# The last layer's modulation vectors as side work of the recurrence instead of block 2's attentions

## The chip, the cores and the metric

The kernel runs on one core of a Trainium2 chip. The metric is the time of one execution in microseconds (us), as the device measures it; lower is better. The engines are named as the profile names them: PE is TensorE (PEld its weight loads), DVE is VectorE, ACT is ScalarE, POOL is GpSimd, SP is SyncE. SP, ACT and POOL also issue DMAs, each in its own order.

## The reference

Two transformer blocks of two layers each are computed in float32 on 256 tokens of width 1024. The second layer of block 1 is a recurrence over 256 context tokens and 256 latent tokens in two directions; the layers of block 2 are attentions followed by a mixture of experts (MoE). Every layer is modulated: a vector `c` is passed through silu and multiplied by a 1024 x 6144 matrix, and the six results of 1024 each shift, scale and gate the layer.

```python
def second_block(x, c, norm1_g, ..., ada_w, ada_b, ...):
    cs = jax.nn.silu(c)
    for l in range(DEPTH):
        mod = (cs @ ada_w[l] + ada_b[l])[:, None, :]
        sh1, sc1, g1, sh2, sc2, g2 = jnp.split(mod, 6, axis=-1)
        h = rms_norm_2(x, norm1_g[l]) * (1.0 + sc1) + sh1
        y = even_mixer_2(h, ...) if l % 2 == 0 else odd_mixer_2(h, ...)
        x = x + g1 * y
        h = rms_norm_2(x, norm2_g[l]) * (1.0 + sc2) + sh2
        x = x + g2 * hier_moe(h, ...)
    return rms_norm_2(x, final_g)
```

`mod` depends on `c` alone, so it can be computed at any time before its layer.

## The kernel before

The program goes through its layers one after the other: block 1's attention layer (`layer0`), the recurrence layer (`odd1`, then `mlp`, both called by `layer1`), and block 2 (`layerB(0)` with `even2`, `layerB(1)` with `odd2`, each followed by `moe`).

The modulation products are **side work**. A product of 512 columns is one unit (`ada_unit`, L191): its weights are 1024 x 512 numbers, 2 MB; eight matmuls of 128 rows each (L203) go to four groups of 32 columns of the PE array, so that up to four of them run side by side; ACT copies the four partial sums (L209); a small product with `sel2` adds them, as four pieces for a column result (L213) or as one for a row result (L217); DVE adds the bias (L255 or L271, and L273 for a norm weight). A layer of block 2 has 12 units (`ada2`, L1408): first four column units, then eight row units, whose results go to DRAM by POOL DMAs (L275).

A generator, `self.side`, yields after every two matmuls. `tick(n)` (L227) takes n such steps wherever the main work calls it, so a unit is four steps. In the recurrence `rw_feat` (L970, the features of two heads) and each of the four steps of `rw_chain` (L1165) call it, with the counts in the table `tk` (L1284). `causal_scores` (L1455) calls it in block 2's attentions. What is left of the generator is finished where `self.do(self.side)` stands: behind the last chain of the recurrence (L856) and in `layerB(1)` (L2005).

The weights come through a ring of buffers (`wload`, L149, and `self.weights(n)`), issued by SP in one order for the whole program. Inside the recurrence the ring has **two buffers of 512 KB** (`self.wn = 2`, `self.weights(2)`, L808 to L811), and the side work has one PSUM bank (`phase((3, 2, 1))`, L818). Behind the recurrence, at L884, a ring of eight buffers of 1 MB begins, which holds first `wo` (the recurrence layer's output matrix, 4 MB) and then the MLP's `w1` and `w2`; block 2 has ten such buffers.

The recurrence is done in four groups (g = 0 to 3), each with features, an inverse on DVE (`rw_inv`), products behind it (`rw_post2` for g = 3) and a chain of four dependent steps. Behind the last chain stand the readout of the second half of the heads (`rw_readout`, L931: a PE product L938, DVE and ACT steps, a PE product L955), the transposes of the result (L898), the product with `wo` (L187 to L189 with `moh`), the residual, and the MLP, which begins with L310.

The order of instructions on each engine is not the order of the code: a scheduler places them when the program is built, with its own estimate of the times. Each engine then runs its list strictly in that order.

Of the kernel before, what the change touches and what calls it, by code (L numbers as in the profile page):

```python
# [110 lines left out]
class K:  # L111
# [55 lines left out]
    def chain(self):  # L167

        prev = [None]

        def mm(*a, **k):
            i = self.nc.tensor.matmul(*a, **k)
            if prev[0] is not None:
                self.after(i, prev[0])
            prev[0] = i
            return i
        return mm
# [486 lines left out]
class L1(K):  # L664
# [21 lines left out]
    def odd1(self, xs, cst, Acol, Bcol):  # L686
# [131 lines left out]
        with self.phase((3, 2, 1), 0) as ph:  # L818
            self.pl = ph.es.enter_context(tc.tile_pool(name="pl", bufs=1, space=PSUM, reuse_waits="tile"))
            gp = ph.pool("gp")  # L820
            St = [self.T(gp, [P, 2, 4, P], f"St{c}") for c in range(2)]
            E3 = [self.T(gp, [P, 4, 65], f"E3{d}") for d in range(2)]
            for c in range(2):
                nc.gpsimd.memset(St[c], 0.0)
                nc.gpsimd.memset(E3[c][:, :, 64 * c:64 * c + 1], 1.0)
            E = dict(E3=E3, kT=kTd, kkn=kknd, rT=rTd, St=St, twl=twl, tal=tal, hpar=hpar, hka=hka, vd=vd,
                     ms=mstrict, mi=mincl, rmask=rmask, yd=yd, Y1=Y1, bon=bon, rkI=rkI, kbd=[self.tc.dram_tile([2, 4, P, 4, P], F32, name=f"kb_dram{g}") for g in range(4)],
                     ard=[self.tc.dram_tile([2, 4, P, 4, P], F32, name=f"ar_dram{g}") for g in range(2)],
                     rbd=[self.tc.dram_tile([2, 4, P, 8, 64], F32, name=f"rb_dram{g}") for g in range(2)])
            st = None  # L830
            self.nq = 4
            F = self.rw_open(0, False, gp)
            for hp in range(4):
                self.rw_feat(hp, gp, E, F)
            for g in range(4):
                N = {"hp": 0}

                def ahead(p):

                    while g < 3 and N["hp"] < 4 and self.pos[g][N["hp"]] <= p:  # L840
                        if N["hp"] == 0:
                            N["F"] = self.rw_open((g + 1) // 2, g % 2 == 0, gp)
                        self.rw_feat(N["hp"], gp, E, N["F"])
                        N["hp"] += 1
                ahead(0)
                self.rw_inv(gp, F)
                ahead(1)
                rest = (self.rw_post2 if g >= self.g2 else self.rw_post)(gp, F)
                st = self.rw_chain(gp, E, F, st, ahead, rest)
                ahead(9)  # L850
                F = N.get("F")
                if F:
                    Fl = F
            F = Fl

            self.do(self.side)  # L856
            E.update(z=z, J=J, sgl=sgl, behind=F["inv"])
            sl = slice(512, 1024)
            nc.gpsimd.dma_start(lng1, A["lng"][sl].partition_broadcast(P))
            nc.gpsimd.dma_start(g21, A["g2"][:, sl])  # L860
            t2 = lambda n: self.T(gp, [P, 512], n, bufs=3 if n in ("BK", "ARx") else 2)
            lng, lnb, g2 = (t2("BK") for _ in range(3))
            nc.gpsimd.dma_start(lng, A["lng"][0:512].partition_broadcast(P))
            nc.gpsimd.dma_start(lnb, A["lnb"][0:512].partition_broadcast(P))
            nc.gpsimd.dma_start(g2, A["g2"][:, 0:512])
            for t in range(2):
                rows = slice(t * P, (t + 1) * P)
                y, y1 = t2("KB"), t2("ARx")
                nc.scalar.dma_start(z[:, t, :], vd[0][rows, 0:512])
                nc.scalar.dma_start(y, yd[0][rows, :])  # L870
                nc.scalar.dma_start(y1, yd[1][rows, :])
                self.rw_bonus(0, t, E, z[:, t, :], lnb)
                self.rw_readout(t, E, y, y1, t2("RB"), lng, g2, z[:, t, :])
            lnb = t2("BK")
            nc.gpsimd.dma_start(lnb, A["lnb"][sl].partition_broadcast(P))
            for t in range(2):
                nc.scalar.dma_start(z1[:, t, :], vd[0][t * P:(t + 1) * P, sl])
                self.rw_bonus(1, t, E, z1[:, t, :], lnb)
# [402 lines left out]
    def q(self, n):  # L1281
        return getattr(self.nc, self.qs[n])

    tk = ((1, 0), (1, 0), (1, 0), (1, 0)), ((1, 2), (1, 2), (1, 2), (1, 2)), (4, 4, 2, 4)  # L1284
    late, g2 = 1, 3
    pos = ((3, 4, 9, 9), (9, 9, 9, 9), (4, 9, 9, 9), (5, 9, 9, 9))

    def layer1(self):
        nc = self.nc
        xs, cst = self.xs[:2], self.xs[2:]  # L1290
        self.at, self.side = "unit", chain(self.gates(1, 0), self.mods(1, 1), self.gates(1, 1), self.ada2(0))
        self.odd1(xs, cst, *self.modc[1, 0])
        self.early2()
        with self.phase() as ph:
            self.ar = ph.pool("ar1")
            self.ws = ph.pool("ws3", 2)
            self.mlp(xs, 1, *self.modc[1, 1], [0, 0], 1)
# [94 lines left out]
class B2(L1):  # L1392
# [600 lines left out]
    def layerB(self, l):  # L1993
        nc, A = self.nc, self.A
        xs = self.xs[:2]
        with self.phase() as ph:
            self.ar = ph.pool(f"arB{l}")
            self.ws = ph.pool(f"wsB{l}", 2)
            Ac, Bc = self.bmods[l]
            if l == 0:  # L2000
                self.at, self.side = "unit", self.ada2(1)
            hT = self.norm_mod_T(xs, Ac, Bc, [0, 0], rs=self.rn)
            mix = (self.even2 if l == 0 else self.odd2)(hT, ph)
            if l:
                self.do(self.side)  # L2005
            else:
                self.flush()
            G = self.T(self.ar, [P, D], "gates", bufs=1)
            self.row(G, f"bda{l}", 2, 0)
            logits = self.out2(mix, A["b_out"] if l == 0 else A["n_out"], xs, G, *self.router(l))  # L2010
        with self.phase(ns2=5) as ph:
            self.ar = ph.pool(f"arM{l}")
            hs = [self.T(self.ar, [P, 2, D], n, F32R) for n in ("mo_hh", "mo_hl")]
            xd = [self.T(self.ar, [P, KT, 256], "mo_xd", bufs=2) for _ in range(1)]
            hb = [self.T(self.ar, [P, D], f"mo_h{t}") for t in range(2)]
            rows = []
            for b in (4, 3, 5):
                rows.append(self.T(self.ar, [P, D], f"mo_row{b}"))
                self.row(rows[-1], f"bda{l}", b, 0)
            if l:  # L2020
                fg = self.T(self.ar, [P, D], "mo_fin")
                nc.gpsimd.dma_start(fg, A["fin_g"].partition_broadcast(P))
                self.fin = fg, hb
            self.rn = self.moe(xs, l, logits, rows, hb, *hs)
            if l:
                for t in range(2):
                    if t:
                        nc.vector.tensor_scalar(hb[t], hb[t], self.rn[t], None, ALU.mult)
                    else:
                        nc.scalar.activation(hb[t], hb[t], AF.Copy, scale=self.rn[t])  # L2030
                    nc.sync.dma_start(self.out[t * P:(t + 1) * P, :], hb[t])
# [54 lines left out]
```

## Time and profile before

| | us |
|---|---|
| median of 3 timed runs | 2259.72 (2257.11 to 2260.31) |
| the profiled execution, its own time | 2250.88 |
| its span, first to last instruction | 2248.9 |
| PE busy in the span | 2075.3 (92%) |
| DVE busy | 1159.6 (52%) |
| ACT busy | 856.6 (38%) |
| mean granted PE clock | 0.936 of 2.4 GHz |

A time of the timeline is counted from the first instruction. Busy shares are means over stages that differ much from each other. A matmul in float32 leaves two records in the trace, so the eight matmuls of a unit are 16 records.

### The profile page before, as it was taken

What the parts mean: (1) busy time and instruction counts of PE and PEld (TensorE: products, weight loads), DVE (VectorE), ACT (ScalarE), POOL (GpSimd) and SP (SyncE); (2) the same over time, 40 slices, a digit from 0 to 9 for tenths busy, and PEclk for the clock granted to TensorE, in tenths of its full rate; (3) what the DMA queues carried; (4) which work ended last, traced back from release to release, by engine and by line L of the source; (5) the groups of instructions that cost most, each with busy time, mean ns of one, the idle gap of its engine ahead of it and who ended that gap; (6) DMA issues with size and microseconds to landing.
All of it is one profiled execution on the core that took longest, in us unless ns stands there. A gap on an engine that the chain in (4) does not pass through costs nothing. (4 is left out here: it accounts for less than half of the span.)

```text
span 2248.9 us, 32827 instructions
## 1 busy us (share of the span) xinstructions
PE 2075.3 (92%) x13114; PEld 1451.2 (65%) x13114; DVE 1159.6 (52%) x2419; ACT 856.6 (38%) x1650; POOL 119.8 (5%) x216
## 2 busy tenths in 40 slices
PE   7999899999989989899997789998998989999897
PEld 4864688888866675685652569987765439646542
DVE  2247543433465536866826265666664236475433
ACT  3334443322352446564432345544452114243211
POOL 0100000000021000001111100000000000010000
PEclk9999999999999998759897889999998999999898
DMA  7448212222332426736886555537464959452494
GB/s 285 142 186 322 76 73 94 94 94 94 113 128 89 140 100 211 228 92 200 263 280 192 177 217 183 187 118 272 171 252 163 386 202 354 156 206 96 179 383 173
DMA packets 124310, 414.53 MB, mean 184 GB/s; under 512 B 20608, under 2 KB 59152, under 8 KB 88432
## 3 DMA queue, kind: packets, MB, share of 16 engines
q1 hardware_dynamic: 59824, 340.03, 41.1%
q10 hardware_dynamic: 55552, 50.95, 7.3%
q0 software_dynamic: 8768, 21.31, 3.1%
q8 instruction: 107, 1.75, 0.3%
q14 instruction: 59, 0.48, 0.1%
HBM read 383.30 MB, written 28.93 MB: 183 GB/s over the span
## 5 line engine op out<-in xcount | busy, mean ns | idle before, releaser
L164 DVE TENSOR_TENSOR wlo<-wraw,whi 128x1024 fp32r<-128x1024 f32 x252 | 308.0, 1225 | 405.6 <-ACT whi L161 398.3
L161 ACT ACTIVATE whi<-wraw 128x1024 fp32r<-128x1024 f32 x252 | 265.4, 1058 | 490.2 <-PE mm L189 234.6
L187 PE MATMUL mm<-hT_h,whi 128*128 128x256 f32 (+1 forms) x832 | 268.2, 333 | 2.3 <-ACT whi L161 2.3
L188 PE MATMUL mm<-hT_l,whi 128*128 128x256 f32 (+1 forms) x832 | 267.3, 328 | 0.0
L189 PE MATMUL mm<-hT_h,wlo 128*128 128x256 f32 (+1 forms) x832 | 242.2, 327 | 0.5 <-DVE wlo L164 0.3
L203 PE MATMUL ada<-wraw,csil 128*32 128x512 f32 x768 | 148.1, 663 | 30.7 <-DMA wraw<-in_bda 19.7
L187 PEld LDWEIGHTS mm<-hT_h,whi 128*128 128x128 f32 x832 | 157.4, 191 | 19.8 <-ACT whi L161 4.0
L188 PEld LDWEIGHTS mm<-hT_l,whi 128*128 128x128 f32 x832 | 158.6, 191 | 14.9
L189 PEld LDWEIGHTS mm<-hT_h,wlo 128*128 128x128 f32 x832 | 149.2, 190 | 16.3 <-DVE wlo L164 1.5
L188 PE MATMUL mm<-wlo,b 128*128 128x512 f32 x384 | 151.3, 394 | 0.1
L189 PE MATMUL mm<-whi,b 128*128 128x512 f32 x384 | 150.8, 393 | 0.0
L1934 PE MATMUL ada<-wraw,mo_xd 128*64 128x512 f32 x512 | 135.5, 599 | 0.0
L187 PE MATMUL mm<-whi,b 128*128 128x512 f32 x384 | 135.1, 393 | 0.0
L310 PE MATMUL tr<-s,x 128*128 128x128 f32 x288 | 57.0, 342 | 50.4 <-DVE s L301 20.0
L188 PE MATMUL mm<-wlo,hT_h 128*128 128x512 f32 (+1 forms) x256 | 98.8, 388 | 1.4 <-DVE wlo L164 1.4
L189 PE MATMUL mm<-whi,hT_l 128*128 128x512 f32 (+1 forms) x256 | 95.9, 388 | 0.0
L187 PE MATMUL mm<-whi,hT_h 128*128 128x512 f32 (+1 forms) x256 | 95.3, 398 | 0.5 <-ACT whi L161 0.4
L310 PEld LDWEIGHTS tr<-s,x 128*128 128x128 f32 x288 | 48.9, 240 | 62.0 <-issue 33.7
L188 PEld LDWEIGHTS mm<-wlo,b 128*128 128x128 f32 x384 | 72.0, 188 | 17.9 <-DVE wlo L164 0.8
L187 PEld LDWEIGHTS mm<-whi,b 128*128 128x128 f32 x384 | 72.0, 188 | 16.6
L189 PEld LDWEIGHTS mm<-whi,b 128*128 128x128 f32 x384 | 72.0, 188 | 16.4
L1934 PEld LDWEIGHTS ada<-wraw,mo_xd 128*64 128x64 f32 x512 | 38.1, 136 | 67.9 <-issue 67.7
(520 smaller groups left out, 3714.6 us busy)
## 6 DMA issues: line engine op xcount, KB each, us to landing
wraw<-in_w SPq DMA_DIRECT2D x64, 1024.0 KB, 4.8
wraw<-in_moe_gu SPq DMA_DIRECT2D x64, 1024.0 KB, 7.8
wraw<-in_ada SPq DMA_DIRECT2D x32, 1024.0 KB, 7.2
wraw<-in_moe_d SPq DMA_DIRECT2D x32, 1024.0 KB, 7.1
wraw<-in_bda SPq DMA_DIRECT2D x48, 512.0 KB, 4.7
wraw<-in_bda SPq DMA_DIRECT2D x24, 1024.0 KB, 4.8
wraw<-in_ada SPq DMA_DIRECT2D x32, 512.0 KB, 4.8
wraw<-in_b_in SPq DMA_DIRECT2D x12, 1024.0 KB, 11.5
```

Source lines behind the costliest of these rows:

```text
L161: nc.scalar.activation(h, src, AF.Copy)
L164: nc.vector.tensor_tensor(l, src, h.bitcast(F32), ALU.subtract)
L187: mm(ps, ah, bh, start=first, stop=False)
L188: mm(ps, ah, bl, start=False, stop=False)
L189: mm(ps, al, bh, start=False, stop=last)
L203: i = nc.tensor.matmul(ps[q:q + 32, :], lhs[:, k, :], raw[:, j % self.wn, :], start=k < nq, stop=k >= 8 - nq, tile_position=(0, q))
L310: nc.tensor.matmul(pt[:, j, :], xs[e + j][:, k * P:(k + 1) * P], dall[:, e + j, :], start=True, stop=True)
L1934: nc.tensor.matmul(pg[64 * e:64 * e + 64, :], xd[:, k, s0:s0 + 64], gu[e](k), start=k == 0, stop=k == KT - 1, tile_position=(0, 64 * e))
```

## The change

The second layer's modulations of block 2, `ada2(1)`, are appended to the generator that the recurrence works off, behind `ada2(0)`. The chain of group 2 takes four steps of the generator per chain step instead of two. A new table `ti` gives ticks behind `rw_inv`, and all its entries are zero. `layerB` no longer starts or finishes a generator, so the ticks of block 2's attentions find nothing to do.

```diff
@@ odd1
                 ahead(0)
                 self.rw_inv(gp, F)
+                self.tick(self.ti[g])
                 ahead(1)
@@ B2
-    tk = ((1, 0), (1, 0), (1, 0), (1, 0)), ((1, 2), (1, 2), (1, 2), (1, 2)), (4, 4, 2, 4)
+    tk = ((1, 0), (1, 0), (1, 0), (1, 0)), ((1, 2), (1, 2), (1, 2), (1, 2)), (4, 4, 4, 4)
+    ti = (0, 0, 0, 0)
@@ layer1
-        self.at, self.side = "unit", chain(self.gates(1, 0), self.mods(1, 1), self.gates(1, 1), self.ada2(0))
+        self.at, self.side = "unit", chain(self.gates(1, 0), self.mods(1, 1), self.gates(1, 1), self.ada2(0), self.ada2(1))
@@ layerB
-            if l == 0:
-                self.at, self.side = "unit", self.ada2(1)
             hT = self.norm_mod_T(xs, Ac, Bc, [0, 0], rs=self.rn)
             mix = (self.even2 if l == 0 else self.odd2)(hT, ph)
-            if l:
-                self.do(self.side)
-            else:
-                self.flush()
```

What the scheduler makes of it is seen in the engines' lists. Behind the first part of `ahead`, lines of the changed kernel have numbers that are higher by one or two (L898 becomes L899, L938 becomes L939).

On PE, at the end of the last chain of the recurrence, the list before goes from the chain's last products (`rbd`, L172) straight to the readout (L938, L955) and the product with `wo` (`moh`):

```order
L172 MATMUL mm_10426<-UV_10343,rbd_10351 64x64
L938 MATMUL tr_10574<-y_1_1152_5818,rwc_4484 128x512
L955 MATMUL tr_10589<-g_1154_5820,sgl_4504 128x512
L187 MATMUL mm_10628<-whi_10634,moh_2148_10555 128x512
L187 MATMUL mm_10629<-whi_10634,moh_2148_10555 128x512
L938 MATMUL tr_10593<-y_1_1152_5818,rwc_4484 128x512
```

In the changed kernel the list goes from the same last product of the chain to side units (`ada`): the fourth column unit, and then the first row unit.

```order
L172 MATMUL mm_10730<-UV_10622,rbd_10630 64x64
L203 MATMUL ada_9429<-wraw_9430,csil_16_107 32x512 x2
L203 MATMUL ada_9429<-wraw_9434,csil_16_107 32x512 x2
L203 MATMUL ada_9429<-wraw_9438,csil_16_107 32x512 x2
L203 MATMUL ada_9429<-wraw_9442,csil_16_107 32x512 x2
L213 MATMUL ada_9523<-sel_4_76,adp_9521 128x2 x4
L203 MATMUL ada_9532<-wraw_9533,csil_16_107 32x512 x2
```

Seven more row units follow it with nothing between them. The last of them ends so, with the transposes, `wo` and the readout behind it:

```order
L203 MATMUL ada_10711<-wraw_10724,csil_16_107 32x512 x2
L217 MATMUL ada_10759<-adp_10757,sel_4_76 2x512
L899 MATMUL tr_10869<-ident_67,z_1149_5815 128x128 x4
L899 MATMUL tr_10876<-ident_67,z_1149_5815 128x128 x4
L187 MATMUL mm_10938<-whi_10944,moh_2244_10865 128x512
L188 MATMUL mm_10938<-wlo_10945,moh_2244_10865 128x512
L187 MATMUL mm_10939<-whi_10944,moh_2244_10865 128x512
L188 MATMUL mm_10939<-wlo_10945,moh_2244_10865 128x512
L939 MATMUL tr_10884<-y_1_1152_5818,rwc_4484 128x512
```

So of the 12 added units three stand among the steps of the last chain and nine behind it, ahead of everything that leads to the MLP. Ahead of the last chain's second step nothing on PE has moved.

On SP, at the same place, the list before goes from the last weights of the side work (`in_bda0`) to `wo` and the MLP's weights:

```order
L151 DMA wraw_1831_8777<-in_bda0 128x1024
L151 DMA wraw_1832_8781<-in_bda0 128x1024
L151 DMA wraw_2172_10632<-in_wo 128x2048
L151 DMA wraw_2177_10666<-in_wo 128x2048
L151 DMA wraw_2182_10700<-in_wo 128x2048
L151 DMA wraw_2187_10734<-in_wo 128x2048
```

In the changed kernel `wo`, and behind it six of the MLP's weights, are issued between the loads of the fourth unit and those of the fifth (`in_bda1`); 30 more loads of the side work follow the last row shown, but for one MLP weight between them:

```order
L151 DMA wraw_2268_10942<-in_wo 128x2048
L151 DMA wraw_2273_10976<-in_wo 128x2048
L151 DMA wraw_1959_9438<-in_bda1 128x1024
L151 DMA wraw_1960_9442<-in_bda1 128x1024
L151 DMA wraw_2278_11010<-in_wo 128x2048
L151 DMA wraw_2283_11044<-in_wo 128x2048
L151 DMA wraw_2336_11220<-in_w1_1 128x2048
L151 DMA wraw_2341_11278<-in_w1_1 128x2048
L151 DMA wraw_2354_11360<-in_w1_1 128x2048
L151 DMA wraw_2359_11418<-in_w1_1 128x2048
L151 DMA wraw_2370_11498<-in_w2_1 128x2048
L151 DMA wraw_1973_9533<-in_bda1 128x1024
```

In block 2's attentions the units are gone from PE's list, 96 matmuls with their 12 sums, and what stood around them closes up. The number of 1 MB loads on SP falls by 24 in block 2, and 48 loads of 512 KB are added in the recurrence.

## Rows read from the trace of the kernel before

**Rows 1.** The page: busy time of the engines, share of the span, instructions.

```profile
PE 2075.3 (92%) x13114; PEld 1451.2 (65%) x13114; DVE 1159.6 (52%) x2419; ACT 856.6 (38%) x1650; POOL 119.8 (5%) x216
```

**Rows 2.** Stretches: us; busy (instructions) of PE, PEld, DVE, ACT, POOL; clock; DMA.

```profile
1211.00:1238.00 27.00, 19.28 (x173) 5.16 (x177) 20.61 (x42) 11.02 (x18) 3.59 (x7) 0.68 0.52 173
1289.40:1331.80 42.40, 30.09 (x113) 22.37 (x113) 30.34 (x46) 21.33 (x35) 0.00 (x0) 0.92 0.73 297
1603.70:1625.00 21.30, 21.30 (x113) 12.29 (x112) 10.64 (x38) 9.94 (x27) 0.00 (x0) 1.00 0.54 198
1625.00:1650.00 25.00, 25.00 (x177) 13.35 (x179) 20.91 (x88) 13.07 (x45) 0.00 (x0) 1.00 0.76 294
1650.00:1665.90 15.90, 15.90 (x106) 9.51 (x99) 8.68 (x23) 7.76 (x25) 1.04 (x2) 1.00 0.66 248
1957.60:1982.30 24.70, 21.74 (x132) 11.05 (x131) 20.86 (x82) 11.50 (x41) 1.02 (x2) 0.82 0.57 213
1982.30:2020.60 38.30, 37.98 (x241) 15.99 (x240) 26.41 (x93) 13.59 (x54) 6.37 (x11) 0.98 0.50 177
2020.60:2029.70 9.10, 8.82 (x50) 4.00 (x49) 7.03 (x26) 3.90 (x18) 0.50 (x1) 1.00 0.46 190
```

**Rows 3.** Timeline of PE, last chain to MLP: start, us, instruction, [idle before].

```profile
1260.47 1.09 PE L1220 MATMUL mm<-rhs,AB 64*64 64x64 f32 x30
...
1288.24 1.15 PE L172 MATMUL mm<-UV,rbd 128*64 128x64 f32 x30 [0.17 <-ACT UV L1224]
1291.88 1.13 PE L938 MATMUL tr<-y,rwc 128*128 128x512 f32 x2 [2.49 <-DVE mol L902]
...
1331.77 2.52 PE L310 MATMUL tr<-s,x 128*128 128x128 f32 x8 [5.04 <-DVE s L301]
```

**Rows 4.** Timeline of PE, side units that follow each other closely, ahead of group 3.

```profile
1215.92 2.76 PE L203 MATMUL ada<-wraw,csil 128*32 128x512 f32 x8 [0.77 <-DVE adb L271]
1221.12 1.05 PE L203 MATMUL ada<-wraw,csil 128*32 128x512 f32 x4 [2.44 <-DMA wraw<-in_bda]
1223.34 1.92 PE L203 MATMUL ada<-wraw,csil 128*32 128x512 f32 x4 [1.17 <-DMA wraw<-in_bda]
1225.96 1.86 PE L217 MATMUL ada<-adp,sel 128*2 128x512 f32 x2 [0.70 <-ACT adp L209]
```

**Rows 5.** SP's 14 side loads from 1199 to 1250: issue to landing.

```profile
DMA to landing us min/median/max: 3.2/4.3/8.1
```

**Rows 6.** Timeline of SP, the last side loads and what follows: start, us, loads.

```profile
1063.71 182.84 SPq L151 DMA_DIRECT2D wraw<-in_bda  x48
1267.97 22.73 SPq L151 DMA_DIRECT2D wraw<-in_wo  x4
```

**Rows 7.** All DMA from 1289 to 1320: packets, MB, mean rate.

```profile
DMA packets 1584, 11.55 MB, mean 373 GB/s; under 512 B 175, under 2 KB 175, under 8 KB 175
```

**Rows 8.** Side matmuls L203, sums L213, sums L217 in both attentions: PE, PEld busy, clock, DMA.

```profile
1603.70:1625.00 21.30, 4.21 (x16) 0.57 (x16) 1.00 0.54 198
...
1650.00:1665.90 15.90, 3.55 (x32) 0.68 (x24) 1.00 0.66 248
...
sum 134.30, PE 27.86 PEld 5.58; mean PE 4.64 PEld 0.93
1603.70:1625.00 21.30, 1.05 (x8) 0.97 (x8) 1.00 0.54 198
...
sum 134.30, PE 4.21 PEld 3.87; mean PE 0.70 PEld 0.65
1650.00:1665.90 15.90, 2.04 (x4) 0.17 (x4) 1.00 0.66 248
...
sum 134.30, PE 8.28 PEld 0.69; mean PE 1.38 PEld 0.12
```

**Rows 9.** Timeline of PE, one side unit's eight matmuls in the first attention.

```profile
1633.62 1.92 PE L203 MATMUL ada<-wraw,csil 128*32 128x512 f32 x16
```

**Rows 10.** Who PE waited for from 1603 to 1672: us, times, longest.

```profile
PE tr L1552 <- DVE ob L1548: 2.4, 2, 2.1
```

## The prediction

> **What bounds the kernel now.** I read the page's busy line first, then stretches of the trace around every place where instructions move, and last the timelines and the loads of the side work. PE is busy 92% of the span and DVE 52% [rows 1], so over the whole program time is PE time. That mean hides three different stages, and the change moves work from one into another.
>
> The first is the recurrence. In its last 80 us PE is often idle: from 1211 to 1238 it works 19.28 of 27.00 us at a granted clock of 0.68, though DMA moves only 173 GB/s [rows 2]. The timeline there says why a side unit is slow [rows 4]: four matmuls, a wait of 2.44 us for the next weights, a pair in 1.05 us, a wait of 1.17 us, a pair in 1.92 us, 0.70 us for ACT, the sum in 1.86 us, 0.77 us for DVE. The same pair takes 1.05 or 1.92 us, so the engine is at 2.4 GHz in one case and at 1.2 GHz in the other. One unit runs from 1215.92 to 1227.82 and the next could begin 0.77 us later: 12.7 us. The weights limit it: a buffer is refilled only when its pair is done, and a load takes 3.2 us at least and 4.3 us at the median from issue to landing [rows 5]. Over the whole recurrence SP issued 48 side loads in 182.84 us, 3.8 us each [rows 6], but most of that lay beside other PE work.
>
> The second stage is the way from the last chain to the MLP. The chain's last product ends at 1289.39, the MLP's first instruction stands at 1331.77 [rows 3]: 42.4 us in which PE works 30.09 us [rows 2], and in which `wo` and the MLP's weights come in, 11.55 MB in 31 us, 373 GB/s or 2.7 us for each MB [rows 7].
>
> The third is block 2's attentions, where the units stand now. A unit's eight matmuls take 1.92 us there [rows 9], all units with their sums 27.86 + 4.21 + 8.28 = 40.35 us of PE, 3.4 us each [rows 8]. PE is busy all the time there and waited 2.4 us in 69 us [rows 10].
>
> **The change part by part.** A unit costs PE the same matmuls wherever it stands; what changes is what lies beside it. The lists (above) give three places.
>
> *Three units among the last chain's steps.* From step 1 (1260.47) to the end (1289.39) the chain takes 28.9 us [rows 3], and its small products leave PE partly idle. A unit needs 3.4 us of PE [rows 8], so the three fill some 10 us of those gaps, but each pair stands in PE's strict order and can wait for a load. If all of it falls into gaps, only late loads are felt: 3 us (say two of the waits of 1.17 us [rows 4]) as the lowest value. If none does, and four of the 12 loads are late by 1.17 us, it is 10 + 5 = 15 us. I take a value between: in the stretch just before, PE was idle for 7.72 of 27.00 us [rows 2]; that share of 28.9 us is 8.3 us of gaps, so 2 us of the units don't fit, and with three waits of 1.17 us that is 5.5 us.
>
> *The fourth column unit and the burst of weights.* Behind the chain SP issues `wo`, four of `w1`, one or two of `w2`, then the fifth unit's first load. In the trace of before, `wo`'s four loads end their issue at 1290.70 [rows 6], since their buffers are free only when the chain is done; so here too they cannot come earlier. With 4 + 4 + 1 MB of them and 1 MB of the fourth unit, 10 MB are ahead of the fifth unit, at 2.7 us each [rows 7] 27 us. PE has for this time only the fourth unit. The lower end is 15 us: the loads share the 16 engines, and a load issued behind the others may land before all of them. The upper end is 30. I take 27, because these bytes moved at just this rate in before.
>
> *Eight row units one behind the other.* Nothing stands between them on PE, so nothing hides their waits. Each of the two buffers serves a unit twice; a round is a pair and a landing. At the fast end that is 2 x (1.05 + 3.2) = 8.5 us, at the slow end 2 x (1.92 + 4.3) = 12.4 us [rows 4, 5], which the 12.7 us of the unit in the trace confirms. Eight units: 68 to 101 us. I take 12.0 us, 96 in all, nearer to the row that did just this. By the clock alone the ends differ by 14 us (8 x 2 x 0.87). The granted clock of 0.68 in that stretch [rows 2] says that it was between the levels. The Trainium skill ("TensorE: Matmul & The Clock Gate", section "HAM oscillation") says that bursts separated by DMA waits drop back to the slow clock, so that each burst begins cold. By it alone the sum would stand 5 us higher, at 12.6 us a unit. On the landing, the Trainium skill ("DMA: Bandwidth & Descriptors", section "Anatomy of one DMA") fits a fixed 2.0 us and bytes over 436 GB/s for DMAs that GpSimd issues, an estimate of 3.2 us for 512 KB. The trace's quickest load agrees with it and the median is 1.1 us above; by the page a unit is 2 x 1.1 us shorter than at the median, and the sum would be some 18 us lower.
>
> *The restart.* The transposes, `wo` and the readout come behind the tail, and so do DVE steps that before stood ahead of the MLP. Its 42.4 us are mostly kept: the second half's readout and `wo` are still to be done. `wo` is on hand by then, a gain of a few us; the features' copies and the loads of `x` come later, a loss. I add 6 us, bounds 2 to 10, the two idle times of 2.49 us and 5.04 us in this stretch [rows 3] being what such a step costs.
>
> *Block 2's gain.* At most the 40.35 us come back. But where DVE is nearly as busy, it is next. In the first attention the first stretch gives back all of its side work, 4.21 + 1.05 = 5.3 us [rows 8], with DVE busy half of it; the middle one (25.00 us, DVE 20.91) at most 4.1 us [rows 2]; the last 3.55 + 2.04 = 5.6 us [rows 8]. In the second attention, the first stretch (24.70 us, DVE 20.86) at most 3.8 us. Then come three steps of a pair of heads with units, 38.30 us, and one without, 9.10 us [rows 2]: 38.30 - 3 x 9.10 = 11.0 us. With a last sum of 1.0 us the total is 15.0 + 15.8 = 31 us. I take 26, since DVE won't be perfectly packed; bounds 15 and 40. MoE needs the same weights as before, and its loads can only start earlier.
>
> Sum: 5.5 + 27 + 96 + 6 - 26 = +108.5 us on the profiled execution's 2250.88, or 2359.4 us. The median of the runs is 8.8 us (0.4%) above that execution, so I predict 2368 us. All terms at their low end give 3 + 15 + 68 + 2 - 40 = +48, all at their high end 15 + 30 + 101 + 10 - 15 = +141.
>
> **The rivals.** *The loads keep pace.* If PE stays at 2.4 GHz and loads land in 3.2 us, a unit takes 8.5 us; the tail is then 68 us. With block 2 giving 31, the sum is 5.5 + 27 + 68 + 6 - 31 = +75.5, 2335 us. For it: with two buffers and nothing else on the queues, DMA is lightly used (173 GB/s). Against it: the unit that did this in before took 12.7 us.
>
> *Block 2 gives little.* If DVE becomes the bound in both attentions the gain is 15 us instead of 26: 5.5 + 27 + 96 + 6 - 15 = +119.5, 2379 us. For it: DVE is busy 20.91 of 25.00 and 20.86 of 24.70 us in two of the stretches. Against it: the other three stretches have DVE busy half to seven tenths of the time.
>
> *The tail runs at block 2's pace (the faster side).* There a unit's matmuls took 1.92 us, with about 1 us for the sum; eight such units cost 23 us, less than the 26 that come back, if the burst is hidden as well. The kernel would then take 2250 to 2255 us. It decides itself at a tail of 26 us in all. It needs the weights on hand: 16 MB, while the ring holds 1 MB. At 373 GB/s, the best rate in the rows, 16 MB alone take 43 us. That speaks against it.
>
> *The change does nothing.* If the moved units only filled idle PE time, what is added would equal what is freed. The lists contradict it: nine units stand with nothing between them.
>
> **How the numbers follow.** I give the forecast 0.77, the pace rival 0.13, little from block 2 0.07, the faster side 0.02, no change 0.01. A difference of 0.2%, 4.5 us, is about what a measurement of this kernel can tell from none. Slower than that: 0.77 + 0.13 + 0.07 = 0.97. The range must reach below the pace rival, as the 27 us of the burst may partly overlap (-7 from 2335 gives 2328), and above the third case with a slow restart and more late loads in the chain (2379 + 17 = 2396). So 2328 to 2396, inside the bounds of all terms at once (2308 to 2401); what is left out on both sides is less than 2 in 10.
>
> **What the changed kernel's profile would show.** The chain's three units: the last product of the chain ends some 5 us later than before. The burst: PE has one unit and then an idle time of some 20 us that a side load ends, while DMA moves some 370 GB/s. The tail: eight sums of row units on PE 12 us apart, with DMA at a third or less of that rate (2 MB in 12 us is 175 GB/s) and a granted clock well under 1. Restart: from the last sum to the MLP's first instruction some 48 us. Block 2: the first attention shorter by 12 to 15 us, the second by 12 to 16, DVE's share up in both.
>
> The prediction is wrong if the sums stand 9 us apart or less (the loads keep pace), if the burst does not hold up the fifth unit, or if the attentions become shorter by much less than 26 us. It is wrong on the sign only if the tail is not in series with the readout.

## The result and the profile after

The changed kernel takes 2390.28 us at the median of four runs (2371.19 to 2397.20), the kernel before 2259.94 us; the ratio is 1.0566 with a 95% interval of 1.0502 to 1.0630. The forecast was 2368 us with a range of 2328 to 2396. The profiled execution took 2386.21 us, 135.3 us more than that of before, where the sum of the prediction stood at 108.5 us.

The page's busy line of the changed kernel [rows 1]:

```profile
PE 2139.7 (90%) x13114; PEld 1464.3 (61%) x13114; DVE 1161.7 (49%) x2419; ACT 857.8 (36%) x1650; POOL 119.7 (5%) x216
```

The number of instructions is the same on every engine, and PE is busy 64 us longer: the same matmuls run at a lower clock or fewer of them side by side. PE is also idle 71 us longer.

Timeline of PE in the changed kernel, from the last chain's second step to the MLP [rows 3, 4] (start, us, instruction, idle time before it and what ended it):

```profile
1262.50 1.15 PE L1221 MATMUL mm<-rhs,AB 64*64 64x64 f32 x32
...
1279.61 1.97 PE L172 MATMUL mm<-St,ard 128*64 128x128 f32 x14 [4.59 <-DMA ard<-ar_dram]
...
1303.98 1.15 PE L172 MATMUL mm<-UV,rbd 128*64 128x64 f32 x30
...
1318.63 1.87 PE L213 MATMUL ada<-sel,adp 128*128 128x2 f32 x8 [0.76 <-ACT adp L209]
1334.80 3.10 PE L203 MATMUL ada<-wraw,csil 128*32 128x512 f32 x8 [14.30 <-DMA wraw<-in_bda]
1340.41 1.92 PE L203 MATMUL ada<-wraw,csil 128*32 128x512 f32 x4 [2.52 <-DMA wraw<-in_bda]
1342.50 1.92 PE L203 MATMUL ada<-wraw,csil 128*32 128x512 f32 x4 [0.17 <-DMA wraw<-in_bda]
1345.18 1.86 PE L217 MATMUL ada<-adp,sel 128*2 128x512 f32 x2 [0.76 <-ACT adp L209]
1347.81 3.10 PE L203 MATMUL ada<-wraw,csil 128*32 128x512 f32 x8 [0.77 <-DVE adb L271]
...
1428.63 1.86 PE L217 MATMUL ada<-adp,sel 128*2 128x512 f32 x2 [0.76 <-ACT adp L209]
...
1473.09 2.52 PE L310 MATMUL tr<-s,x 128*128 128x128 f32 x8 [5.04 <-DVE s L301]
```

Nearly all of the loss is between these rows. The chain ends at 1305.13, 15.7 us later than before; 2.0 us of that were there at its second step. The first row unit begins at 1334.80, 29.7 us behind the chain, after an idle time of 14.30 us that a side load ends. The eight row units end at 1430.49: 95.7 us, 12.0 us each. From there to the MLP it is 42.6 us, as before (42.4). Together the MLP begins 141.3 us later.

The same three stretches by window: us; busy (instructions) of PE, PEld, DVE, ACT, POOL; clock; DMA share, GB/s [rows 2]:

```profile
1305.10:1334.80 29.70, 7.65 (x26) 2.43 (x25) 5.06 (x6) 5.79 (x7) 0.00 (x0) 0.56 1.00 403
1334.80:1430.50 95.70, 61.60 (x145) 6.39 (x146) 6.10 (x9) 4.78 (x8) 9.18 (x18) 0.66 0.54 177
1430.50:1473.10 42.60, 31.07 (x121) 23.50 (x121) 28.07 (x47) 18.47 (x31) 0.51 (x1) 0.90 0.26 95
```

First all 16 DMA engines are full (share 1.00, 403 GB/s) and PE mostly stands; then PE works through the units at a clock of 0.66 while DMA moves 177 GB/s. What PE waited for in the second of them (us in total, times, longest):

```profile
PE ada L203 <- DMA wraw<-in_bda: 36.9, 21, 14.3
PE ada L217 <- ACT adp L209: 6.1, 8, 0.8
PE ada L203 <- DVE adb L271: 5.4, 7, 0.8
```

Without the first wait of 14.3 us, which lies ahead of the stretch, loads cost 22.6 us of the 95.7. With PE's own 61.6 us, the 6.1 for ACT and the 5.4 for DVE the stretch is accounted for.

Block 2's attentions in the changed kernel, and under them a row of before that the groups do not show (same columns); the first row answers to the three of the first attention in [rows 2], 62.20 us:

```profile
1745.70:1793.90 48.20, 45.28 (x267) 30.02 (x266) 37.05 (x141) 27.92 (x90) 1.14 (x2) 1.00 0.24 84
2090.40:2141.20 50.80, 46.66 (x250) 25.85 (x249) 39.29 (x156) 19.59 (x85) 0.00 (x0) 0.80 0.00 1
2141.20:2173.00 31.80, 29.23 (x112) 14.04 (x113) 16.05 (x59) 7.80 (x33) 0.00 (x0) 0.56 0.00 1
```

```profile
1957.60:2018.90 61.30, 58.02 (x359) 25.84 (x358) 46.40 (x171) 24.43 (x92) 7.39 (x13) 0.92 0.52 190
2018.90:2038.50 19.60, 19.05 (x118) 9.63 (x115) 14.94 (x56) 8.23 (x35) 0.50 (x1) 1.00 0.28 108
```

The first attention became 14.0 us shorter. The second gave back 10.5 us up to the last scores but one, and then lost 12.2 us: the same matmuls without the units took 31.80 us instead of 19.60, at a granted clock of 0.56 instead of 1.00, so mostly at 1.2 GHz. PE is "busy" 92% of that time and its longest wait there is 1.16 us, yet the clock is low. From the MLP's first instruction to the end of the span the gain was 5.8 us: 0.1 in the MLP, 11.8 in block 2's first layer, minus 6.1 in its second. So the spans differ by 141.3 - 5.8 = 135.5 us (the executions' own times by 135.3).

### The profile page after: what moved, and what is told of

It reads as the page before. It is cut to its first block, busy times and chain, and to the rows that moved or that the text cites. A ratio compares the mean times of both kernels' runs of the same rounds, so it can differ in the third digit from the quotient of the medians.

```text
span 2384.4 us, 32902 instructions
## 1 busy us (share of the span) xinstructions
PE 2139.7 (90%) x13114; PEld 1464.3 (61%) x13114; DVE 1161.7 (49%) x2419; ACT 857.8 (36%) x1650; POOL 119.7 (5%) x216
## 5 line engine op out<-in xcount | busy, mean ns | idle before, releaser
L203 PE MATMUL ada<-wraw,csil 128*32 128x512 f32 x768 | 187.5, 715 | 83.1 <-DMA wraw<-in_bda 66.5
L203 PEld LDWEIGHTS ada<-wraw,csil 128*32 128x32 f32 x768 | 25.9, 115 | 164.1 <-DMA wraw<-in_bda 94.7
L209 ACT ACTIVATE adp<-ada 128x512 f32<-128x512 f32 x48 | 28.6, 596 | 203.1 <-PE ada L203 188.9
L187 PEld LDWEIGHTS mm<-whi,b 128*128 128x128 f32 x384 | 72.0, 188 | 16.7
```

The costliest lines, as they stand in the source:

```text
L187: mm(ps, ah, bh, start=first, stop=False)
L203: i = nc.tensor.matmul(ps[q:q + 32, :], lhs[:, k, :], raw[:, j % self.wn, :], start=k < nq, stop=k >= 8 - nq, tile_position=(0, q))
L209: nc.scalar.activation(part[kr], ps[kr], AF.Copy)
```

## The experiments

Each median is of the runs of that kernel, each ratio is to the kernel before run beside it on the same chip. Single executions of one kernel lie up to 30 us apart, in one case 56, so stretches of a trace are compared before medians are.

**Block 2's gain alone.** The kernel before with the second layer's units left out (its `layerB(1)` reads the first layer's vectors):

```diff
-            if l == 0:
-                self.at, self.side = "unit", self.ada2(1)
-            Ac, Bc = self.bmods[l]
+            Ac, Bc = self.bmods[0]
...
```

> The kernel before, without the second layer's 12 units at all (left out: its modulations; the layer takes the first layer's vectors), so the recurrence is that of before and only block 2's gain shows. My theory after the result: the first attention gives back about 14 us, and the second almost nothing, because PE falls to 1.2 GHz in its last third once the side units are gone; total 5 to 14 us faster than before, 2246 to 2255 us, and a granted clock near 0.5 to 0.75 in the 30 us at the end of the second attention. Rival, the prediction's term: both attentions give back what DVE leaves, 26 to 31 us, 2229 to 2234 us, with the clock at 1.0. Second rival: the loss in the second attention comes from something the moved work does earlier in the changed kernel; then here too 26 us or more.

Measured: 2242.79 us, ratio 0.9960 (0.9928 to 0.9992): 9 us faster, 2 to 16 by the interval. Its second attention, from the first transpose to the last (90.50 us), by window:

```profile
1966.60:2057.10 90.50, 86.03 (x454) 48.15 (x454) 57.87 (x199) 30.40 (x112) 0.00 (x0) 0.85 0.07 24
```

The first layer of block 2 took 12.5 us less than before, the second 0.7 us more. So the second layer gives back nothing here either, where nothing was moved into the recurrence; the second rival falls, and so does the term of 26 us. The place differs from what I expected: the low clock lay ahead of 2010 us, mostly in the first half of that attention, and its last third ran at 1.00.

**Does idle PE work bring the clock back?** The changed kernel with units without loads, copies and sums in the second attention:

```diff
+            if l:
+                self.at, self.side = "unit", self.filler(6)
...
+    def filler(self, n):
+        for u in range(n):
+            ps = self.T(self.pa, [P, 512], "ada")
+            for k in range(8):
+                q = 32 * (k % 4)
+                i = self.nc.tensor.matmul(ps[q:q + 32, :], self.cs2[:, k, :], self.xs[k % 2][:, 0:512], start=k < 4, stop=k >= 4, tile_position=(0, q))
...
```

> The changed kernel with six idle units in the second attention: eight products each of 128 rows from data at hand into a bank that nobody reads; no loads, no copies, no sums. It adds about 12 us of PE work and leaves nothing out. Clock theory: the last pairs of heads run at 2.4 GHz again, the 31.8 us from the third last scores to the output product become 20 to 23 us, and the whole is 3 to 12 us faster than the changed kernel, 2378 to 2387 us. Rival, PE or DVE time: the added products cost up to their own time, 0 to 12 us slower, 2390 to 2402 us.

Measured: 2389.34 us (2386.25 to 2391.57), the time of the changed kernel. Two stretches of its trace, the first attention (which is the changed kernel's own) and the second, first transpose to last:

```profile
1731.60:1793.60 62.00, 59.51 (x267) 36.66 (x266) 38.28 (x141) 28.08 (x90) 1.22 (x2) 0.72 0.19 66
2100.20:2201.90 101.70, 95.36 (x518) 49.70 (x518) 58.47 (x202) 29.50 (x109) 0.00 (x0) 0.85 0.06 22
```

My expectation failed: the second attention did not become shorter than the changed kernel's 97.5 us, and its clock was 0.85. The first row says something else. The first attention, in which nothing differs from the changed kernel, had a clock of 0.72 here and took 62.00 us with the same 267 records that took 48.20 us above. It is the exception: in the other eight profiled executions without units there, the first attention had a clock of 1.00. But it shows that the clock can fall there in one execution and not in another. Fillers of this kind do not bring the second attention to the 0.96 of before.

**The burst of weights.** The changed kernel with all later weights behind the last side load on SP:

```diff
             self.do(self.side)
+            self.hold = self.lw
...
-        (self.wq or self.nc.sync).dma_start(t, ap)
+        i = (self.wq or self.nc.sync).dma_start(t, ap)
+        if self.hold is not None:
+            self.after(i, self.hold)
+        self.lw = i
...
```

> The changed kernel with the loads of wo and the MLP's weights placed behind the last side load on SP. If the burst of these loads holds up the fifth unit, the way from the chain's end to the first row unit's matmuls falls from 29.7 us to 12 to 17 us, and some 5 to 12 us come back at the restart because wo (4 MB at 2.7 us each) now lands after the tail: in all 3 to 12 us faster than the changed kernel. Rival: the fifth unit waits for something else (its bank, the buffers); then the way stays near 30 us and the restart makes the kernel 8 us slower.

Measured: 2356.77 us, ratio 1.0469 (1.0411 to 1.0528). The profiled execution was the longest of the five (2387.20; the others 2331.41 to 2359.21). Its way from the chain to the MLP:

```profile
1322.74 3.14 PE L207 MATMUL ada<-wraw,csil 128*32 128x512 f32 x8 [0.26 <-DVE bA L259]
...
1410.77 1.86 PE L221 MATMUL ada<-adp,sel 128*2 128x512 f32 x2 [0.75 <-ACT adp L213]
...
1459.56 2.53 PE L314 MATMUL tr<-s,x 128*128 128x128 f32 x8 [6.32 <-DVE s L305]
```

The chain ended at 1311.26 there. The first row unit follows 11.5 us behind it instead of 29.7, and no load ends its wait any more. The eight units took 89.9 us, the restart 46.9 us (+4.3): 148.3 us from the chain to the MLP instead of 168.0. The burst is the cause of the 14.30 us wait. The gain of 20 us on this way is above the 3 to 12 us I gave: the way to the first row unit shrank by 18.2 us, the eight units by 5.8, which I had not priced, and the restart took 4.3 of it back, less than I had expected.

What made this execution long lies in block 2's second attention, first transpose to last:

```profile
2089.10:2204.40 115.30, 110.58 (x454) 58.52 (x453) 58.89 (x199) 30.73 (x112) 0.00 (x0) 0.62 0.05 19
```

That is 17.8 us more than in the changed kernel (97.50 us at 0.79) with the same work, at a granted clock of 0.62.

**The tail's loads.** The changed kernel with one load of 512 KB for a row unit instead of four (three quarters of those weights are left out):

```diff
-                if j % self.wn == 0:
+                if j % self.wn == 0 and not (self.few and hf + j):
...
+        self.few = l == 1
         for b in (2, 3, 4, 5):
             yield from self.row2(l, b)
+        self.few = False
```

> The changed kernel with only one load of 512 KB for each of the eight row units of the second layer instead of four (its other matmuls take the same buffer: the wrong three quarters of those weights are left out). If the two-buffer ring sets the tail's pace, a unit takes 4.5 us at 2.4 GHz to 7.2 us at 1.2 GHz (matmuls 1.92 or 3.84, copy 0.76, sum 1.02 or 1.86, bias 0.77) instead of 12.0, the eight 36 to 58 us instead of 95.7, the whole 40 to 60 us faster than the changed kernel, 2330 to 2350 us. Rival: PE's slow clock and the chain of copy, sum and bias set it; then a unit stays above 9 us and the whole gains under 25 us.

Measured: 2325.70 us, ratio 1.0332 (1.0271 to 1.0393). Its tail, on PE:

```profile
1336.87 3.64 PE L203 MATMUL ada<-wraw,csil 128*32 128x512 f32 x16 [14.31 <-DMA wraw<-in_bda]
1341.28 1.87 PE L217 MATMUL ada<-adp,sel 128*2 128x512 f32 x2 [0.77 <-ACT adp L209]
...
1368.72 1.92 PE L203 MATMUL ada<-wraw,csil 128*32 128x512 f32 x16 [0.77 <-DVE adb L271]
1371.42 1.02 PE L217 MATMUL ada<-adp,sel 128*2 128x512 f32 x2 [0.78 <-ACT adp L209]
...
1384.41 1.02 PE L217 MATMUL ada<-adp,sel 128*2 128x512 f32 x2 [0.78 <-ACT adp L209]
```

Eight units took 48.6 us, 6.1 us each, half of 12.0. So half of the tail is the units' loads. That the two buffers are the reason, and not the loads' number as such, was not tried; the DMA engines were not full in the tail (share 0.54). The rows show that the price is more than waiting: with the weights at hand all eight matmuls stand together, four side by side, 1.92 us at 2.4 GHz (3.64 at the lower clock), while in pairs they need 4 x 1.05 or 4 x 1.92.

**Loads or matmuls in the last chain.** The same edit for the four column units instead of the row units:

```diff
+        self.few = l == 1
         yield from self.mods2(l)
+        self.few = False
```

> The changed kernel with one load of 512 KB instead of four for each of the four column units of the second layer (their other matmuls take the same buffer: the wrong three quarters of those weights are left out); PE's work and order stay. The way from the last chain's second step to its end took 28.9 us in the kernel before and 42.6 us in the changed one. If the side loads beside the chain's own loads delay it (a chain's operand of 256 KB landed in a median of 2.7 us before, 6.7 us after), it falls to 30 to 36 us. Rival: the units' matmuls in PE's strict order delay it, and with them the moment when the chain's buffers come free; then it stays at 38 us or more.

Measured, in a single execution: 2361.08 us. The way from the chain's second step (1248.92) to its end (1289.10) by window, here and, in the second fence, in the changed kernel and, in the third, before:

```profile
1248.90:1289.10 40.20, 37.11 (x531) 22.66 (x530) 5.11 (x12) 10.82 (x19) 3.12 (x6) 0.96 0.51 159
```

```profile
1262.40:1305.10 42.70, 33.89 (x483) 21.66 (x484) 4.10 (x9) 9.61 (x17) 2.12 (x4) 0.92 0.64 208
```

```profile
1260.40:1289.40 29.00, 20.92 (x417) 17.80 (x416) 4.23 (x9) 8.81 (x15) 2.62 (x5) 0.94 0.43 137
```

It stayed at 40.2 us, but as a test it is weak: with quicker loads the scheduler put 88 records of L203 (5.5 units) into the stretch instead of 50 (3). PE's idle time is read better: 3.1 us here, 8.8 us in the changed kernel, 8.1 us before. What PE waited for, in the same order (us in total, times, longest):

```profile
PE ada L203 <- DMA wraw<-in_bda: 3.0, 2, 2.4
```

```profile
PE mm L172 <- DMA ard<-ar_dram: 4.6, 1, 4.6
PE ada L203 <- DMA wraw<-in_bda: 4.1, 4, 1.5
```

```profile
PE mm L172 <- DMA UV<-v_dram: 3.8, 2, 2.1
PE mm L1220 <- ACT rhs L1214: 1.7, 2, 1.0
PE mm L172 <- DMA ard<-ar_dram: 1.6, 1, 1.6
PE mm L172 <- DVE St L1248: 0.8, 1, 0.8
PE mm L172 <- ACT UV L1224: 0.2, 1, 0.2
```

Before, all 8.1 us are the chain's own waits. In the changed kernel 4.6 us of such waits are left, so the units filled 3.5 us of the gaps, and 4.1 us of waits for side loads came with them. The 4.6 us are one wait for an operand (`ard`) that landed 6.7 us after its issue at 1272.89, 10.4 us behind the second step. In the run with one load for a row unit, whose chain holds the same units, such waits were 3.0 us. Here the operand was issued 10.5 us behind the second step (1259.39), landed within 4.3 to 4.8 us, and PE, busy with a side unit meanwhile, did not wait for it. So the chain's gaps can be filled where the side loads are few: in this one execution no wait of its own is left. The stretch stays long because PE is busy 37.11 of its 40.20 us.

**The place in the recurrence.** The changed kernel with 32 steps of the generator behind the first group's inverse:

```diff
-    ti = (0, 0, 0, 0)
+    ti = (32, 0, 0, 0)
```

> The changed kernel with 32 steps of the generator, eight units, behind the first group's inverse on DVE; four units are left behind the last chain instead of nine. If only the place decides, five units of the tail go, 5 x 12 = 60 us, and the eight early units cost between nothing and 6 us each in a stretch in which PE is granted 1.2 GHz and DMA moves 43 to 145 GB/s: 2335 to 2375 us, 15 to 55 us faster than the changed kernel. Rival: the early units cost as much as in the tail; then it stays within 12 us of it.

Measured: 2290.79 us, ratio 1.0172 (1.0121 to 1.0222): some 90 us faster than the changed kernel by the two ratios (0.0394 of 2260), more than I gave it, with four units behind the chain instead of nine. The chain ended at 1301.44, no later than in the changed kernel, so the eight early units cost nothing that shows there.

**Versions that might beat both.** Four column units moved there, two row units left in the first attention, six in the second:

```diff
-        self.at, self.side = "unit", chain(self.gates(1, 0), self.mods(1, 1), self.gates(1, 1), self.ada2(0), self.ada2(1))
+        self.at, self.side = "unit", chain(self.gates(1, 0), self.mods(1, 1), self.gates(1, 1), self.ada2(0), self.mods2(1))
-    tk = ((1, 0), (1, 0), (1, 0), (1, 0)), ((1, 2), (1, 2), (1, 2), (1, 2)), (4, 4, 4, 4)
-    ti = (0, 0, 0, 0)
+    tk = ((1, 0), (1, 0), (1, 0), (1, 0)), ((1, 2), (1, 2), (1, 2), (1, 2)), (4, 4, 2, 4)
+    ti = (16, 0, 0, 0)
...
+            blks = (3, 4, 5) if l else (2,)
+            self.at, self.side = "unit", chain(*(self.row2(1, b) for b in blks))
...
+            self.do(self.side)
```

> A version that might beat both: the second layer's four column units in the recurrence behind the first group's inverse (16 steps there, the chain of group 2 with two steps as before), two row units in the first attention, six in the second as before. The first attention should give back 4/6 of 14 us, 9 us; the second keeps its units and its time. If the four early units are hidden, 5 to 10 us faster than the kernel before; if each costs 3 us of PE, no difference that can be told.

Measured: 2231.87 us, ratio 0.9926 (0.9897 to 0.9955), faster than the kernel before by some 17 us.

The same with six units there (`mods2(1)` and `row2(1, 2)`, `ti = (24, 0, 0, 0)`) and none in the first attention:

> The same with six units behind the first group's inverse (24 steps), none in the first attention, and six in the second as before. The first attention gives back 14 us. If the early units are hidden, 8 to 15 us faster than the kernel before; if each costs 3 us of PE, 0 to 5 us slower or the same.

Measured: 2236.72 us, ratio 0.9940 (0.9907 to 0.9972). And with eight (`row2(1, 3)` too, `ti = (32, 0, 0, 0)`), four left in the second attention:

> Eight units of the second layer in the recurrence (32 steps behind the first group's inverse), none in the first attention, four in the second. None stands behind the last chain. If eight early units are hidden as four are, the first attention gives back 14 us and the kernel takes 2225 to 2235 us, no worse than the version with four. Rival: the second attention with four units instead of six falls to 1.2 GHz in part and gives back 5 to 20 us: 2235 to 2250 us.

Measured: 2248.69 us, ratio 0.9985 (0.9956 to 1.0014): no gain that can be told. Its last chain took 44.9 us from its second step to its end, so, it seems, the added units push later ones into the chain. Eight moved units win less than four; between four and six the intervals tell no difference. That asks whether the moved units won anything. The kernel before, with nothing moved, but 16 steps of its own generator behind the first inverse:

```diff
                 self.rw_inv(gp, F)
+                if g == 0:
+                    self.tick(16)
```

> The kernel before with 16 steps of its generator behind the first group's inverse, and nothing else: the same 20 units of the recurrence, four of them earlier, and the same 12 in block 2. If the gain of the version with four column units moved there (0.74%, 17 us, of which the first attention explains 9) comes in part from where the units stand in the recurrence, the last group's stage no longer waits for side loads and this is 5 to 12 us faster than before. Rival: the order of the units in the recurrence is worth nothing, and it stays within 4 us of before.

Measured: 2225.42 us (2215.74 to 2233.96), ratio 0.9877 (0.9834 to 0.9919): 28 us faster than before, the lowest median of all kernels, and more than twice what I gave it. Two stretches of it, and under them the same two of before:

```profile
920.00:1000.00 80.00, 65.69 (x483) 41.84 (x481) 60.80 (x170) 47.75 (x114) 3.02 (x6) 0.87 0.76 237
...
1230.00:1264.10 34.10, 25.14 (x508) 22.09 (x508) 4.83 (x8) 10.08 (x18) 1.06 (x2) 0.85 0.50 162
```

```profile
920.00:1000.00 80.00, 74.47 (x431) 59.98 (x431) 61.15 (x172) 48.82 (x118) 0.00 (x0) 0.61 0.45 133
...
1230.00:1289.40 59.40, 46.68 (x812) 30.21 (x811) 17.79 (x35) 21.41 (x36) 7.87 (x15) 0.86 0.55 173
```

From 920 to 1000 PE has 52 records more, 64 of them side matmuls, and is busy 8.8 us less, because its clock is 0.87 instead of 0.61; the stage ends as early as before. The added units raised it: in these 80 us the clock was 0.54 to 0.62 in the seven profiled executions without early units, and 0.80 to 0.95 in the five with them. At the other end the chain is over at 1264.03 instead of 1289.39; its last side matmul stands at 1194 instead of 1255. The version with four moved units begins its MLP at 1323.06 in its profiled execution, 8.7 us earlier than before, and its first layer of block 2 is 8.1 us shorter; here the MLP begins at 1305.32, 26.5 us earlier, and block 2 is no shorter. So in these executions the order was worth some 26 us, and the four moved units took some 18 us of that and gave back 8. The medians point the same way, but the two intervals overlap a little. That this order is the best, or that all of the 28 us come from the last group's stage, was not tried.

## Why the prediction was right

The sign, the place and the two largest terms held. The chain and block 2 were off, both towards a faster kernel, and the restart made up for part of it. That the range still held, 6 us below its upper end, was in part luck: block 2's gain came out below the 15 us that the prediction gave as its least, and its own sign of being wrong (attentions shorter by much less than 26 us) was seen. What left room for it was the upper end, taken from the rival in which block 2 gives little. By the prediction's steps, predicted and measured in the profiled executions:

| step | predicted | measured |
|---|---|---|
| ahead of the last chain's second step | 0 | +2.0 |
| three units among the last chain's steps | +5.5 | +13.7 |
| fourth unit and the burst | +27 | +29.7 |
| eight row units | +96 | +95.7 |
| restart | +6 | +0.2 |
| block 2 (with 0.1 of the MLP) | -26 | -5.8 |
| sum | +108.5 | +135.5 |

*The chain.* The step "2 us of the units don't fit" was mis-sized, by two of its terms. The gaps to be filled were put at 8.3 us, and 3.5 were filled; the rest is one wait for an operand of the chain, which landed after 6.7 us, against 4.3 to 4.8 where the side loads were fewer. The units' PE work was put at 10 us by block 2's 3.4 us a unit, and PE's busy time grew by 13.0, since their matmuls came in pairs or fours and not all eight together. The late loads were right: 3.5 us predicted, 4.1 measured. Together 13.0 - 3.5 + 4.1 = 13.6.

*The burst.* Right in cause and size; with the weights held back, the way shrank to 11.5 us. The working counts a load of 1024 KB as 1 MB; at 373 GB/s ten of them take 28 us and not 27. Nor did all of `wo` wait for the chain's end: its first load was issued at 1302.39, 2.7 us ahead of it. The lower end of 15 us, other loads overtaking, did not occur: the fifth unit's first two loads were issued from 1316.66 on and landed 17.5 to 18.0 us later.

*The tail.* 12.0 us a unit, as priced from one unit of before. Its working made it up of two rounds of a pair and a landing, and left out the copy, the sum and the bias; the size came from the row, not from that working. Measured are, for a unit, 7.7 us of PE work, 2.8 us of waits for loads and 1.4 us for ACT and DVE. With one load instead of four a unit takes 6.1 us, so the loads are half of it; but the direct waits are 22.6 us of 95.7, and the rest of that half is matmuls that can't stand four abreast, with a clock of 0.66 in all (0.70 with one load). The Trainium skill ("TensorE: Matmul & The Clock Gate", section "HAM oscillation") tells of a kernel in which each burst of matmuls behind a DMA wait starts at the low clock; the tail's 0.66 agrees in part, since pairs took 1.05 us and 1.92 us in turn, so not every burst began cold.

*The restart.* The 6 us were not there: `wo` had landed early, and the 42.6 us hardly differ from the 42.4. With `wo` late, in the run with the weights held back, it was 46.9.

*Block 2.* The first attention gave 14.0 us (15.0 at most by the prediction). The second was the step that failed: "DVE is next" sees two bounds, PE and DVE, but the bound that came was PE's clock. In that attention of the changed kernel DVE is busy 58.12 of 97.50 us, and the rival in which DVE becomes the bound came near the measured time for a reason that did not occur. The second attention, first transpose to last, before, in the changed kernel, and in the run with fewer loads for the column units:

```profile
1972.80:2065.80 93.00, 89.41 (x528) 46.52 (x528) 63.95 (x211) 34.08 (x118) 7.38 (x13) 0.96 0.37 134
2104.60:2202.10 97.50, 91.63 (x455) 50.86 (x454) 58.12 (x199) 30.51 (x112) 0.00 (x0) 0.79 0.06 22
2061.20:2176.40 115.20, 110.49 (x455) 58.35 (x454) 58.87 (x199) 30.72 (x112) 0.00 (x0) 0.62 0.05 19
```

The six profiled executions without units there took 88.5 us at 0.88 (changed kernel with eight early units), 90.5 at 0.85 (units left out), 91.3 at 0.85 (one load for a row unit), 97.5 at 0.79 (changed kernel), 115.2 and 115.3 at 0.62 (one load for a column unit; weights held back). The four with six units took 93.0 to 96.7 us at 0.93 to 0.96. So without the units the best execution won 4.5 us on the kernel before and the worst lost 22.3; none came near the 15.8 us of the prediction. The two groups' clocks do not overlap, so the lower clock goes with the missing units. What of a unit holds the clock up is open: the fillers, its matmuls without loads, copies and sums, left it at 0.85, and no run had the units' loads, copies and sums without their matmuls.

## What to carry to other kernels

Side work is cheap where its pieces stand ahead of their need and beside an engine that is working anyway; the same piece costs 12 us when nothing else stands beside it to cover its waits. Idle time of an engine inside a chain of dependent steps is room only in part: side work that brings loads can make the chain's own loads late, and here 3.5 of some 8 us were filled. Work that is taken out of a stretch can lower the clock of what is left there, so its busy time is not what comes back. And before moving work from one stage to another, try its order within the stage: here the order alone was worth 28 us, and no version that also moved units did better.

## What the runs showed of the hardware

PE can be busy nine tenths of a stretch, with no wait over 1.2 us, and be granted 1.2 GHz: in the changed kernel's 31.80 us at 0.56, and from 920 to 1000 before, at 0.61. More PE work can leave such a stretch no longer: with four units added, the latter ran at 0.87 and PE's busy time fell from 74.5 to 65.7 us, and over all profiled executions its clock was 0.54 to 0.62 without such units and 0.80 to 0.95 with them. And the same instructions get different clocks in different executions: the first attention without units took 48.20 us at 1.00 in the changed kernel and 62.00 us at 0.72 in the run with fillers, and the second took 88.5 us at 0.88 in one run and 115.3 us at 0.62 in another.
